# Expert outputs scattered to token rows, h1 kept in SBUF and the smallest experts last: one encoder block on one core

## The chip, the cores and the metric

The kernel runs on one core of one Trainium2 chip. The metric is the device time of one execution in microseconds (us), the median of three runs. An execution computes one layer for 512 tokens of width 1024, all in float32 (the large matmuls of the first half are done in three passes of a split format). Five engines run their own instruction streams and meet at semaphores: PE (matmul, with PEld, its weight loads), DVE (vector), ACT (scalar), POOL (GpSimd) and SP, which here only issues DMAs. DMAs are issued from the queues of SP, ACT and POOL and carried by the core's 16 DMA engines. PSUM holds matmul results, SBUF the working tiles (128 partitions), DRAM the inputs and two buffers of the kernel's own.

## The reference

Before the part that is changed: `h = LayerNorm(x)`, one projection, a gated MLP branch and a gated delta rule branch, and `h1 = LayerNorm(alpha*h + mix)`. What matters here is what follows:

```python
def _hier_moe(x, w_rg, b_rg, w_re, b_re, w1, w3, w2):      # x: h1, 512 x 1024
    pg = softmax(xt @ w_rg + b_rg); grp = argmax(pg, -1)    # 1 of 4 groups
    le = (xt @ w_re + b_re).reshape(n_tok, 4, 8)[own group] # 8 experts of it
    top_v, top_i = lax.top_k(le, 2)                         # 2 of the 8
    gate = p_grp * softmax(top_v, -1)
    ...
    def expert_block(xb, e):
        return (silu(xb @ w1[e]) * (xb @ w3[e])) @ w2[e]
    out = zeros.at[tok].add(gate * y)                       # sum of a token's 2 experts
h = LayerNorm(alpha * h1 + out)                             # LN2: the output
```

Both experts of a token lie in one group. There are 32 experts of 1024 x 512 (w1, w3) and 512 x 1024 (w2): 6.3 MB each. Which tokens an expert gets is data. Worked out from the reference's inputs, the 1024 pairs of token and expert fall very unevenly: two experts get none, the largest 130, 126, 104 and 94.

## The kernel before

**First half, to about 680 us.** Projections, gating and the delta rule (eight heads) are written through a recording layer (`Rec`) that sets the order by costs; all its instructions carry line 214. During the heads SP also fills `y_dram` (line 1519), the DRAM buffer for the experts' outputs, with zeros: 48 DMAs of 512 KB (lines 1578 to 1580). Then `out_ln1` (line 948) multiplies by `w_o`, adds the residual, normalizes without gain and bias, and writes these rows of h1 to `h1_dram`; the router (`Router`, lines 1044 to 1276) finds each token's two experts as the tiles come by.

**Order of the experts.** `Router.order` (line 1088) sets the order of the 32 blocks from the counts in the first 256 tokens: experts in a fixed sequence, those that look empty moved ahead of the last four. The first three are known beforehand. With these inputs the last four blocks have 126, 13, 130 and 19 tokens, and the two experts without tokens stand side by side as blocks 24 and 25.

**Experts.** `Experts.run` (line 1313) goes through the blocks, written out in full. Each expert's weights come as six loads of 1 MB on SP's queue (`load_big`, line 391) into a ring of 18 buffers `raw` (lines 1608 and 1621); a load is issued when its buffer is free, and is skipped by a condition where the expert has no token. For block b, in program order: POOL gathers the tokens of block b+2 from `h1_dram` by an indirect DMA (`fetch`, line 1394; 64 rows always, 96 more under an If); PE multiplies up (line 1447) in parts: a small one of up to 32 tokens and up to two of 64, each under an If; ACT and DVE form silu times product (lines 1454, 1455); PE turns the next block's tokens (line 1422); PE multiplies block b-1 down (line 1475); and `store_y` (line 1478) copies the results from PSUM (DVE the small part, line 1483; ACT the large ones, line 1485) and POOL stores them with five plain DMAs, each under a condition, to the expert's own 160 rows of `y_dram` (lines 1487, 1492). Stores to `y_dram` wait for one another where the framework sees that they could overlap. Between these steps `Router.rest` (line 1153) puts in DVE work for the gates, for places of outputs (`yi`) and for experts with over 160 tokens (`nov`, `oi`; none here).

**End.** `finish_rows` (line 1004) loads h1 again (4 x 512 KB) and the rows of gain and bias (4 x 512 KB) with SP, and forms alpha*h1 with gain and bias. A loop over overflow blocks follows (line 1661), which these inputs never enter. `finish` (line 1022) gathers the two expert rows of every token (8 indirect DMAs of 128 rows, line 1028), adds them with their gates (DVE, line 1034), normalizes (statistics in lines 357 to 375, then lines 1037 to 1039), and stores the four tiles of 128 tokens (line 1040).

Of the kernel before, what the change touches and what calls it, by code (L numbers as in the profile page):

```python
# [34 lines left out]
NYROW = (32 + 6) * NB + 64  # L35
# [5 lines left out]
NPRE = 3  # L41

# [217 lines left out]
class K:  # L260
# [4 lines left out]
    def consts(self, S, M, W):  # L265
# [78 lines left out]
        iota("eidnb", [128, E], [[NB, E]], 0, 0)  # L344
        iota("seq", [128, E], [[1, 8], [8, 4]], 0, 0)
# [6 lines left out]
        iota("tok", [128, NT], [[128, NT]], -2 * T, 1)  # L352
        c["tok16"] = S.tile([128, NT], F16, name="tok16")
# [650 lines left out]
    def finish_rows(self, h1_dram):  # L1004
# [6 lines left out]
        self.raws, self.nraw = free[8:14], 0  # L1011
# [10 lines left out]
    def finish(self, W, r, y_dram):  # L1022
        nc, a = self.nc, self.a
        v, act = nc.vector, nc.scalar
        ys = self.ys
        for t in range(NT):
            for k in range(2):
                nc.gpsimd.indirect_dma_start(out=ys[2 * t + k], out_offset=None, in_=y_dram,  # L1028
                                             in_offset=bass.IndirectOffsetOnAxis(ap=r.yi[:, k, t:t + 1], axis=0),
                                             bounds_check=NYROW - 1, oob_is_err=False)  # L1030
        for t in range(NT):
            f = self.h1f[t]
            for k in range(2):
                v.scalar_tensor_tensor(out=f, in0=ys[2 * t + k], scalar=r.g[:, t, k:k + 1], in1=f,  # L1034
                                       op0=OP.mult, op1=OP.add)
# [3 lines left out]
            (nc.gpsimd if t < 3 else v).tensor_tensor(out=f, in0=f, in1=self.l2b, op=OP.add)  # L1039
            nc.sync.dma_start(out=a["out"][t * 128:(t + 1) * 128, :], in_=f)  # L1040
# [3 lines left out]
class Router:  # L1044
# [3 lines left out]
    def __init__(self, nc, tc, S, W, P, cst, lg, persist):  # L1048
# [9 lines left out]
        self.idx = persist.tile([128, 2, E], I32, name="idx")  # L1058
        self.cum = S.tile([128, NT, E], F32, name="cum")
# [28 lines left out]
    def order(self):  # L1088
# [3 lines left out]
        for t in range(2):  # L1092
            q = W.tile([128, 2, E], BF, name="oq")
            v.tensor_tensor(out=q, in0=bc(cst["iota"][:, 0:E], 2, 1), in1=bc(self.ek[:, :, t], E, 2), op=OP.is_equal)
            for k in range(2):
                nc.tensor.matmul(self.cps[:, NT], cst["ones_bf"], q[:, k], start=t + k == 0, stop=t + k == 2)
        f = W.tile([128, E], F32, name="of_")
        v.tensor_scalar(f.rearrange("p (j g) -> p j g", g=4), self.cps[:, NT].rearrange("p (g j) -> p j g", g=4),
                        0.0, None, op0=OP.is_gt)
        v.memset(f[:, 0:NPRE], 1.0)  # L1100
        r = W.tile([128, E], F32, name="or_")
# [42 lines left out]
    def sort(self):  # L1144
        nc, v = self.nc, self.nc.vector
        for i, n in enumerate((NA, NB - NA)):
            v.tensor_scalar(self.idx[0:n, i], self.sps[i][0:n], 2.0 * T, None, op0=OP.add)
# [588 lines left out]
```

## Time and profile before

| | |
|---|---|
| median of 3 runs | 1244.05 us (1242.74 to 1249.01) |
| profiled execution, its own time | 1246.53 us |
| its span, first to last instruction | 1244.8 us |
| PE, DVE, ACT, POOL busy | 83%, 52%, 32%, 16% of the span |
| moved by DMA | 296.10 MB, mean 238 GB/s |

Times in the profile count from the start of the span. The page's 40 slices are 31 us each; a digit is a share in tenths. A view of stages (windows) has a row for each stretch of time: its length, the busy time of PE, PEld, DVE, ACT and POOL with the number of instructions, the granted PE clock, the busy share of the 16 DMA engines, and GB/s. A view of waits gives who waited for whom, the total in us, how often, and the longest. Groups of instructions name the line, engine, operation and tiles (out<-in), shape and count, then busy us and mean ns of one, then idle time ahead and what ended it. `raw` is the ring of weight buffers, which the end of the kernel reuses for h1, rows and gathered outputs.

### The profile page before, as it was taken

The numbers are of one execution on the slowest core, as the hardware profiler recorded it, in microseconds if no ns is written. First come the engines' busy times: TensorE is split into PE (matmuls) and PEld (weight loads), VectorE is DVE, ScalarE is ACT, GpSimd is POOL, SyncE is SP. The second block draws the span as 40 slices with busy tenths as digits, with TensorE's granted clock in tenths as the row PEclk, the third lists the DMA queues.
The fourth block names the chain that finished last, engine by engine and source line by source line (L and its number), as shares of the span: only waits on it lengthen the run. The fifth ranks groups of instructions, "written<-read, shape, count | busy, mean of one in ns | idle before, by whom it ended". The sixth has DMA issues, their size and how long they took to land. (4 is left out here: it accounts for less than half of the span.)

```text
span 1244.8 us, 19415 instructions
## 1 busy us (share of the span) xinstructions
PE 1039.3 (83%) x6880; PEld 687.0 (55%) x6880; DVE 646.2 (52%) x1356; ACT 403.1 (32%) x844; POOL 193.5 (16%) x377
## 2 busy tenths in 40 slices
PE   4999999999999999999999588787877586579810
PEld 2888788867777777667887333443333242234300
DVE  7566444567667777754865444533223232433246
ACT  6333355444555455435431311111111111211111
POOL 1000100212212132200001101111111101111043
PEclk9999999999999999999999698997979897799965
DMA  5422533899221121114672799999999999999832
GB/s 172 153 84 69 160 95 110 284 341 362 70 68 58 45 68 52 34 52 152 238 308 91 295 385 409 391 411 400 414 390 415 399 414 399 377 387 387 349 115 111
DMA packets 76899, 296.10 MB, mean 238 GB/s; under 512 B 9328, under 2 KB 34176, under 8 KB 53216
## 3 DMA queue, kind: packets, MB, share of 16 engines
q1 hardware_dynamic: 66672, 272.13, 58.0%
q0 software_dynamic: 7504, 17.20, 4.3%
q10 hardware_dynamic: 2592, 4.99, 1.2%
q8 instruction: 87, 1.43, 0.5%
q14 instruction: 44, 0.36, 0.1%
HBM read 277.36 MB, written 50.35 MB: 263 GB/s over the span
## 5 line engine op out<-in xcount | busy, mean ns | idle before, releaser
L214 PE MATMUL psi<-hTh,lo 128*128 128x512 f32 x448 | 183.0, 410 | 1.6 <-DVE lo L214 1.6
L214 PE MATMUL psi<-hTh,hi 128*128 128x512 f32 x448 | 183.5, 413 | 0.9 <-ACT hi L214 0.5
L214 PE MATMUL psi<-hTl,hi 128*128 128x512 f32 x448 | 183.1, 411 | 0.0
L1455 DVE TENSOR_TENSOR h<-h,u 128x640 f32<-128x640 f32 x32 | 26.3, 822 | 279.2 <-ACT h L1454 267.2
L214 DVE TENSOR_TENSOR lo<-raw,hi 128x1024 fp32r<-128x1024 f32 x74 | 91.3, 1234 | 79.6 <-ACT hi L214 78.9
L1447 PE MATMUL u<-raw,xs 128*32 128x256 f32 x1472 | 102.1, 426 | 29.8 <-DMA raw<-in_w 28.2
L214 ACT CAST hi<-raw 128x1024 fp32r<-128x1024 f32 x74 | 77.5, 1047 | 117.3 <-PE psi L214 100.2
L1447 PE MATMUL u<-raw,x 128*64 128x512 f32 x448 | 103.6, 618 | 5.9 <-PEq L1387 2.9
L214 PEld LDWEIGHTS psi<-hTh,lo 128*128 128x128 f32 x448 | 84.4, 188 | 21.3 <-issue 3.9
L214 PEld LDWEIGHTS psi<-hTh,hi 128*128 128x128 f32 x448 | 84.6, 189 | 20.3 <-issue 2.8
L214 PEld LDWEIGHTS psi<-hTl,hi 128*128 128x128 f32 x448 | 84.4, 189 | 17.2 <-issue 1.6
L1447 PEld LDWEIGHTS u<-raw,xs 128*32 128x32 f32 x1472 | 50.9, 120 | 73.4 <-DMA raw<-in_w 38.6
L1454 ACT ACTIVATE h<-u 128x640 f32<-128x640 f32 x32 | 22.6, 705 | 204.5 <-PEq L1389 160.9
L1447 PEld LDWEIGHTS u<-raw,x 128*64 128x64 f32 x448 | 35.5, 143 | 68.6 <-issue 60.0
L1475 PE MATMUL y<-raw,hT 128*64 128x512 f32 x224 | 60.1, 672 | 11.5 <-PEq L1387 9.2
L1475 PE MATMUL yz<-raw,hT 128*32 128x256 f32 x736 | 55.2, 437 | 16.4 <-PEq L1427 5.9
L1464 ACT COPY hT<-t 128x128 f32<-128x128 f32 x32 | 8.5, 266 | 184.0 <-PE t L1461 172.7
L1483 DVE COPY ysmall<-yz 32x256 f32<-32x256 f32 x128 | 53.3, 417 | 16.8 <-PE yz L1475 15.3
L214 DVE SCALAR_TENSOR_TENSOR acc<-xp,cols,acc 128x512 f32<-128x512 f32 x72 | 54.7, 760 | 4.7 <-ACT acc L214 3.5
L1492 POOL DMA_DIRECT2D y_dram<-ylarge x128 | 19.5, 155 | 194.1 <-DMA y_dram<-ysmall 114.8
L1475 PEld LDWEIGHTS yz<-raw,hT 128*32 128x32 f32 x736 | 26.3, 121 | 35.7 <-issue 18.0
L1422 PE MATMUL t<-ident,mh 64*128 64x64 f32 x256 | 23.5, 237 | 25.8 <-PEq L1389 20.0
(437 smaller groups left out, 1864.9 us busy)
## 6 DMA issues: line engine op xcount, KB each, us to landing
raw<-in_w SPq DMA_DIRECT2D x192, 1024.0 KB
raw<-in_wt SPq DMA_DIRECT2D x73, 512.0 KB
y_dram<-zero SPq DMA_DIRECT2D x48, 512.0 KB
y_dram<-ylarge POOLq DMA_DIRECT2D x128, 128.0 KB
raw<-in_wv SPq DMA_DIRECT2D x8, 512.0 KB
raw<-in_wo SPq DMA_DIRECT2D x4, 1024.0 KB
y_dram<-ysmall POOLq DMA_DIRECT2D x32, 128.0 KB
vt<-in_x SPq DMA_DIRECT2D x4, 512.0 KB
```

The source lines that it names most:

```text
L214: op._ins = getattr(getattr(self.nc, op.attr), op.name)(*map(real, op.args), **{k: real(x) for k, x in op.kw.items()})
L1422: nc.tensor.transpose(self.t[0][:, k * NA:k * NA + NA], r[0][:, k * 128:k * 128 + 128], ident[0:NA, 0:NA])
L1447: self.nc.tensor.matmul(self.u[q * r:(q + 1) * r, NP if p is None else p, 0:c], x[:, k, r0:r0 + r], self.raw[b, k // 2][:, o:o + c], start ...
L1454: self.nc.scalar.activation(out=h, in_=u[:, :, 0], func=AF.Silu)
L1455: self.nc.vector.tensor_mul(out=h, in0=h, in1=u[:, :, 1])
L1464: self.nc.scalar.copy(out=x[:, n], in_=self.t[1][:, 0:128])
L1475: self.nc.tensor.matmul(y[q * r:(q + 1) * r, 0:c], t[:, i, j * r:(j + 1) * r], self.raw[b, 4 + k // 2][:, o:o + c], start=k == 0, stop=k == 3)
L1483: nc.vector.tensor_copy(out=small[:, q], in_=self.y0[q * 32:(q + 1) * 32, 0:256])
L1492: nc.gpsimd.dma_start(out=dst[:, q * 512:(q + 1) * 512], in_=large[q * 64:(q + 1) * 64, p], cond=n > 32 + 64 * p)
```

## The change

**Places of rows.** The router now sorts pairs (token and slot, 2*512) instead of tokens; `rows` computes for each block the pair's row for the small part (`itail`) and for the large parts (`islot`), with an index out of bounds where there is no token.

**Stores.** `y_dram` becomes 1024 rows, two for each token side by side. `store_y` issues three indirect DMAs (scatters) from POOL, for every block and without conditions, and declares that no two have a row in common. `yo_dram` is used only in a fallback.

**Buffers.** The four tiles of h1 stay in SBUF; the second part of the ring shrinks from 9 to 8 buffers (17 in all), and from block 25 on four more are taken out for the tail. There is one landing buffer for large gathers instead of two, and the large gather of block b+2 is issued after the next block is turned.

**Order.** `Router.order` ranks by a key: experts that look empty come about ten places later than their turn, and the smallest expert of each group, by the counts of the first 256 tokens, goes to the end. With these inputs the last four blocks have 2, 18, 5 and 15 tokens; a token has no two of them, since they are of four groups. Their outputs are not stored: they are kept in one tile (`Y`) or read from PSUM.

**Tail.** From block 25 on, `Tail` does the end's work between the blocks' steps: gain and bias as 4 KB rows spread by PE, alpha*h1 with gain and bias, then at block 29 plain loads of `y_rows` (four of 1 MB, from ACT's queue, two rows of a token in one partition), the sums with gates, LN2 and the stores of all four tiles of 128 tokens, the tokens of the last four experts wrong in them. Those tokens (40 pairs here) are handled apart in a tile `F` of 128 rows: their h1 and their other expert's row are gathered, the last four outputs added, LN2 done, and their rows scattered over the output at the very end.

**Fallback.** A flag is the sum of three counts: two of the last four experts in one group, a last expert with over 32 tokens, an expert with over 160. If it is positive, an If loads `y_rows` over to `yo_dram`, runs the last four experts again with their stores, and ends as before. With these inputs it is 0.

**Zeros.** 8 DMAs of 512 KB instead of 48.

The diff, cut to its core:

```diff
@@ Router.order
+        mn = W.tile([128, 4], F32, name="om_")
+        v.tensor_reduce(out=mn, in_=gj(sc), axis=AX.X, op=OP.min)
...
+        v.scalar_tensor_tensor(out=f, in0=lt, scalar=128.0, in1=f, op0=OP.mult, op1=OP.add)
+        eq = W.tile([128, E, E], BF, name="oeq")
+        v.tensor_tensor(out=eq, in0=bc(f, E, 1), in1=bc(f, E, 2), op=OP.is_lt)
@@ Experts.run
         for b in range(nb + 1):
             if b + 2 < nb:
-                for i in range(2):
-                    self.fetch(b + 2, i)
+                self.fetch(b + 2, 0)
+            if tail and b >= RT:
+                tail(b, 0)
             if b < nb:
                 self.parts(b, self.up)
-                load(4)
+                if tail and b == RT:
...
+                    self.spare, kk.raws, kk.nraw = kk.raws[0:4], kk.raws[4:], 0
+                else:
+                    load(4)
                 self.gate(b)
...
-            if b:
-                self.store_y(b - 1)
+            if b and not (tail and b == nb):
+                self.store_y(b - 1, tail)
             next(more, None)
+            if tail and b >= RT:
+                tail(b, 1)
@@ Experts.store_y
+    def scatter(self, out, idx, src):
+        x = self.nc.gpsimd.indirect_dma_start(out=out, out_offset=bass.IndirectOffsetOnAxis(ap=idx, axis=0), in_=src,
+                                              in_offset=None, bounds_check=out.shape[0] - 1, oob_is_err=False)
...
+            self.tc.declare_no_dep(x.ins, group="rows", reason="no two have a row in common")
...
-        nc.gpsimd.dma_start(out=self.y_dram[ds(row + r0, 32), :], in_=small.rearrange("r q n -> r (q n)"), cond=d > 0)
+        self.scatter(self.y_dram, itail, small.rearrange("r q n -> r (q n)"))
         for p in range(NP):
-            for q in range(2):
-                nc.gpsimd.dma_start(out=dst[:, q * 512:(q + 1) * 512], in_=large[q * 64:(q + 1) * 64, p],
-                                    cond=n > 32 + 64 * p)
+            self.scatter(self.y_dram.rearrange("r (q n) -> (r q) n", q=2), islot[:, p], large[:, p])
@@ Tail.__call__ (new; RT = 25, E = 32)
+        elif (b, at) == (RT + 4, 0):
+            kk.behind(self.load(0), ex.stores)
+            self.load(1)
+        elif (b, at) == (RT + 4, 1):
+            self.add(0, 1)
+            self.load(2)
+            self.load(3)
+            self.gather(self.O, self.y_dram, r.lother, 2 * T)
+        elif (b, at) == (RT + 5, 0):
+            self.apply((0, 1), self.stats(0, 1))
+        elif (b, at) == (RT + 5, 1):
+            self.add(2, 3)
...
+        elif (b, at) == (RT + 6, 0):
+            self.m = self.stats(2, 3)
+        elif (b, at) == (RT + 6, 1):
+            self.apply((2, 3), self.m)
...
+        elif (b, at) == (E, 2):
...
+            (rs, mean), = self.stats(F)
+            self.norm(F, rs, mean)
+            x = g.indirect_dma_start(out=kk.a["out"], out_offset=bass.IndirectOffsetOnAxis(ap=r.lidx, axis=0), in_=F,
+                                     in_offset=None, bounds_check=T - 1, oob_is_err=False)
@@ build
-    close(OT, OP_, RP, OS, MM, RH, OH)
+    close(OT, OP_, RP, OS, MM, OH)
-    kk.add_raws(ER2, 9)
+    kk.add_raws(ER2, 8)
-    kk.finish_rows(h1_dram)
+    with tc.If(flag > 0):
+        kk.finish_rows(h1_dram, y_dram, yo_dram, ex.stores)
...
+    with tc.manual_schedule():
+        tail(E, 2)
```

Three places of the built programs show what moves. First POOL in the loop over the experts, from one block's stores to the next gathers, before (`mh` is the landing buffer of tokens, `cnti` the counts, ISA a condition):

```order
L1487 ISA
L1487 DMA y_dram<-ysmall 32x1024
L1492 ISA
L1492 DMA y_dram<-ylarge 64x512
L1401 DMA mh<-h_dram,idx 64x1024
L1380 TENSOR_LOAD cnti
L1398 COMPARE_AND_BRANCH
L1401 DMA mh<-h_dram,idx 96x1024
```

The same place now:

```order
L1549 DMA y_rows<-ysmall,itail 1024x1024
L1549 DMA y_rows<-ylarge,islot 2048x512 x2
L1468 DMA mh<-h_dram,idx 64x1024
L1454 UNCONDITIONAL_BRANCH
L1456 UNCONDITIONAL_BRANCH
L1494 UNCONDITIONAL_BRANCH
L1447 TENSOR_LOAD cnti
L1465 COMPARE_AND_BRANCH
L1468 DMA mh<-h_dram,idx 96x1024
```

The row of the conditioned large store stands four times in a block before; now there are three scatters without a condition, and the large gather has moved behind the turn of the next block (the branch of line 1494). Second, SP at the end of the experts, before, with the last weight load and what follows it:

```order
L1387 UNCONDITIONAL_BRANCH
L1389 UNCONDITIONAL_BRANCH
L399 ISA
L399 DMA raw_5392<-in_w 128x2048
L1013 DMA raw_5393<-h_dram 128x1024 x2
L1015 DMA raw_5395<-in_rows 128x1024 x2
L1659 TENSOR_LOAD nov
L1661 COMPARE_AND_BRANCH
L1040 DMA out<-raw_5393 128x1024 x2
```

And now (`h1s` are the tiles of h1):

```order
L401 DMA raw_5355<-in_w 128x2048
L401 ISA
L401 DMA raw_5356<-in_w 128x2048
L1691 DMA out<-h1s_4428 128x1024
L1691 DMA out<-h1s_4429 128x1024
L401 ISA
L401 DMA raw_5361<-in_w 128x2048
L1691 DMA out<-h1s_4430 128x1024
L1691 DMA out<-h1s_4431 128x1024
L1861 TENSOR_LOAD flag
L1862 COMPARE_AND_BRANCH
```

The loads of h1 and of the rows are gone from SP, and the stores of the output stand ahead of the flag, the first two of them ahead of the last weight load. Third, ACT's queue in the last blocks now, from the spread of LN2's rows on (before, ACT issued no DMA among the experts):

```order
L1648 ACTIVATE raw_5357<-t_5366 128x512
L1656 DMA raw_5359<-y_rows 128x2048
L1656 DMA raw_5360<-y_rows 128x2048
L1454 UNCONDITIONAL_BRANCH
L1456 UNCONDITIONAL_BRANCH
L1521 ACTIVATE h<-u 128x640
L1494 UNCONDITIONAL_BRANCH
L1465 UNCONDITIONAL_BRANCH
L1498 UNCONDITIONAL_BRANCH
L1531 COPY hT<-t_5366 128x128
L1532 COPY hT<-t_5365 128x512
```

The loads of the expert rows stand on ACT ahead of a block's silu (line 1521), so that ACT reaches the silu only when the scatters before them have landed.

More of the change, by code (lines that the diff above doesn't have):

```diff
@@ L1010, in finish_rows @@
         self.h1f, (g, b, self.l2g, self.l2b), self.ys = half[0:4], half[4:8], half[8:16]
-        self.raws, self.nraw = free[8:14], 0
+        self.raws, self.nraw = free[8:], 0
+        for i, y in enumerate(self.ys):
+            sl = slice(i * 128, (i + 1) * 128)
+            x = nc.sync.dma_start(out=y, in_=y_dram[sl, :])
+            if i == 0:
+                self.behind(x, stores)
+            nc.sync.dma_start(out=yo[sl, :], in_=y)
         for t in range(NT):
@@ L1344, in run @@
         next(more, None)
[L1345 to L1346 removed]
+        self.fetch(0, 1)
         next(more, None)
@@ L1476, in down, with late @@
                                       self.raw[b, 4 + k // 2][:, o:o + c], start=k == 0, stop=k == 3)
-    def store_y(self, b):
-        nc, row = self.nc, self.blocks[b][0]
-        small = self.yp.tile([32, 4, 256], F32, name="ysmall")
-        large = self.yp.tile([128, NP, 512], F32, name="ylarge")
+    def late(self, i):
+        return self.Y[32 * i:32 * i + 32].rearrange("r (q n) -> r q n", q=4)
+    def scatter(self, out, idx, src):
+        x = self.nc.gpsimd.indirect_dma_start(out=out, out_offset=bass.IndirectOffsetOnAxis(ap=idx, axis=0), in_=src,
+                                              in_offset=None, bounds_check=out.shape[0] - 1, oob_is_err=False)
+        if self.behind:
+            self.kk.behind(x, self.behind)
+            self.behind = None
+        if out.tensor.name == self.y_dram.tensor.name and not self.tracked:
+            self.tc.declare_no_dep(x.ins, group="rows", reason="no two have a row in common")
+            self.tc.add_to_no_dep_group("rows", x.ins)
+        self.stores.append(x)
@@ L1482, in store_y @@
+    def store_y(self, b, tail=None):
+        nc, (itail, islot) = self.nc, self.blocks[b][0]
+        i = b - (E - NL)
+        late = tail and i >= 0
+        small = self.late(i) if late else self.yp.tile([32, 4, 256], F32, name="ysmall")
         for q in range(4):
             nc.vector.tensor_copy(out=small[:, q], in_=self.y0[q * 32:(q + 1) * 32, 0:256])
+        if late:
+            return
+        large = self.yp.tile([128, NP, 512], F32, name="ylarge")
         for p in range(NP):
             nc.scalar.copy(out=large[:, p], in_=self.y[p])
-        n, d, r0 = (self.n(b, ET.Pool, i) for i in range(3))
```

336 lines of the change are left out of this document (237 added, 99 removed).

## The prediction

> **What bounds the kernel now.** I read the page's slices first, then the stages, the waits, the chain. The slices:
>
> ```profile
> PE   4999999999999999999999588787877586579810
> DMA  5422533899221121114672799999999999999832
> ```
>
> Up to slice 22 PE is full; from slice 24 to slice 37 DMA stands at 9 and PE below it. Then both go, while the execution lasts two slices more. The stages (columns as told above):
>
> ```profile
> 682.00:696.00 14.00, 9.40 (x57) 7.32 (x56) 6.43 (x24) 2.78 (x6) 0.86 (x2) 0.91 1.01 418
> 732.00:1050.00 318.00, 246.19 (x2303) 115.08 (x2300) 116.11 (x243) 52.97 (x105) 46.60 (x131) 0.89 1.02 405
> 1050.00:1070.00 20.00, 12.65 (x86) 5.30 (x82) 7.32 (x14) 3.77 (x8) 2.57 (x12) 0.89 0.87 339
> 1165.00:1175.00 10.00, 6.85 (x113) 4.32 (x108) 4.14 (x10) 2.53 (x5) 0.51 (x1) 0.99 1.02 408
> 1175.00:1180.00 5.00, 5.00 (x35) 1.94 (x29) 2.08 (x5) 0.00 (x0) 0.67 (x5) 0.68 0.49 195
> 1180.00:1200.00 20.00, 7.34 (x61) 2.73 (x55) 5.17 (x7) 4.80 (x8) 2.81 (x9) 0.80 0.19 43
> 1200.00:1245.00 45.00, 0.00 (x0) 0.00 (x0) 30.78 (x38) 4.96 (x4) 23.07 (x15) 0.50 0.40 140
> ```
>
> The experts from 732 us on run at the pace of their weights: DMA 1.02, 405 GB/s, PE 246 of 318 us. An expert has 6.29 MB, so 15.5 us. PE needs far less where an expert has up to 32 tokens, as its up and down show, and more for the large ones (two large parts):
>
> ```profile
> 1129.83 3.66 PE L1447 MATMUL u<-raw,xs 128*32 128x256 f32 x64
> 1164.46 1.93 PE L1475 MATMUL yz<-raw,hT 128*32 128x256 f32 x32 [0.42 <-PEq L1427]
> 1149.44 13.95 PE L1447 MATMUL u<-raw,x 128*64 128x512 f32 x64
> 1177.15 7.59 PE L1475 MATMUL y<-raw,hT 128*64 128x512 f32 x32
> 1185.40 1.93 PE L1475 MATMUL yz<-raw,hT 128*32 128x256 f32 x32
> ```
>
> So a small block is 5.6 us of PE and a large one 27; only a large block at the very end puts PE after the stream. The last load of weights landed at about 1167: DMA is full to 1175 and for 49% of the next 5 us, to 1177.4, and the last that it carries are the loads of h1 and of the rows, queued on SP behind the weights:
>
> ```profile
> 1151.16 8.98 SPq L1013 DMA_DIRECT2D raw<-h_dram  x4
> 1162.32 7.83 SPq L1015 DMA_DIRECT2D raw<-in_rows  x4
> raw<-h_dram SPq DMA_DIRECT2D x4, 512.0 KB
> ```
>
> Eight of half a MB are 4.19 MB, 10.3 us at 405, so the weights were in at 1167.1. The 77.7 us after that are PE's rest of the block of 130 tokens, to 1187.3 (the last of the matmul rows), then the chain of waits:
>
> ```profile
> 1187.54 10.02 DMA y_dram<-ylarge
> 1204.80 6.04 DMA raw<-y_dram,yi
> 1237.83 1.23 DVE raw L1039
> ```
>
> A wait until stores have landed, gathers of all outputs, LN2 of four tiles, a store. So the end of the profile is set first by the stream's bytes, then by what hangs on the last expert's outputs.
>
> **The change part by part.** I sum when the weights have landed now, and what follows them.
>
> *Bytes in the stream.*
>
> ```profile
> q0 software_dynamic: 7504, 17.20, 4.3%
> DA<-g_dram POOLq DMA_DIRECT2D x8, 256.0 KB
> raw<-in_w SPq DMA_DIRECT2D x192, 1024.0 KB
> ```
>
> Loads run ahead of PE by as many buffers as the ring has, so one fewer (17, not 18) is 1 MB less in SBUF when the experts start: +1.05 MB. The four taken out at block 25 cost no bytes, since 13 MB ahead of PE is still two experts. The four plain loads of `y_rows` come at blocks 29 and 30, while weights still flow, on ACT's queue but through the same 16 engines: +4.19. Two of four output stores stand ahead of the last weight load: +1.05. The gathers for the 40 apart pairs, two of 4 KB each: +0.33. Stores fall: POOL's queue moved 17.20 MB, less 2.10 (`DA`), 4.19 (1024 tokens gathered) and 4.19 (8 end gathers) leaves 6.7 MB of stores, whole parts of 32 or 64 rows, 0.86 of it after 1180 (43 GB/s for 20 us); now only 984 real rows go, 4.03 MB: −1.8. Together +4.8 MB; at 405 GB/s 11.9 us. The loads of h1 and rows lay behind the weights and go for nothing. Weights have landed at 1167.1 + 11.9 = **1179.0**.
>
> The rate itself is bound by two rows: 339 GB/s in a stretch with stores, 418 in one without. If scatters left no mark, the 447 us from 732 to 1179 would become 433 (× 405/418, −14); if they marked it twice as much, +14. I take none, since the same rows go to the same memory in both kernels. The Trainium skill ("DMA: Bandwidth & Descriptors", Where 436 GB/s comes from) says that for transfers between HBM and SBUF the HBM side binds at about 358 GB/s; by it the 4.8 MB would be 13.4 us, 1.5 more. The trace disagrees: 405 for 318 us with one core at work.
>
> *Order.* All blocks from 26 on are at most 18 tokens, so PE, 5.6 us of 15.5, waits for weights when the last land. PE's 20 us behind them go. Those large blocks now stand as blocks 22 and 24, and PE's arrears there (27 − 15.5 us each) are absorbed within three small blocks.
>
> *POOL.* Three scatters take the place of five conditioned stores per block. Rows for their price:
>
> ```profile
> L1401 POOL DMA_INDIRECT mh<-h_dram,idx x38: 931/986/1457, 699.7 to 1140.2; - x38
> L1028 POOL DMA_INDIRECT raw<-y_dram,yi x8: 989/1458/2068, 1200.2 to 1212.2; - x8
> POOL y_dram L1492 <- DMA y_dram<-ysmall: 114.8, 19, 9.3
> ```
>
> Scatters at 1 to 2 us are 3 to 6 us per block, gathers 2 to 3, of 15.5; the 115 us in which POOL waited for stores goes, but they lay beside a stream that set the pace. The large gather, moved behind the next block's turn, has still more than a block of time. Cost 0 while that cover lasts; without it, rival 2.
>
> *Zeros, router.* 40 of 48 zero DMAs go from 214 to 307 us:
>
> ```profile
> 214.00:307.00 93.00, 90.28 (x495) 68.06 (x494) 56.16 (x116) 41.58 (x96) 19.89 (x29) 1.00 0.96 324
> 640.00:682.00 42.00, 40.95 (x220) 31.56 (x219) 23.03 (x87) 7.51 (x11) 4.06 (x4) 1.00 0.39 140
> ```
>
> PE is busy 90.3 of those 93 us, so at best 2.7 us come from it; I take 0, as DVE and ACT end PE's waits there. The router's order chain is some 2.6 us longer on DVE, which has 19 of 42 us free: 0, at most +2.
>
> *Tail between blocks.* The sums, statistics and norms of four tiles are the DVE work of the old end:
>
> ```profile
> L1034 DVE SCALAR_TENSOR_TENSOR raw<-raw,g,raw 128x1024 f32<-128x1024 f32 x8 | 10.0, 1269 | 3.8 <-DMA raw<-y_dram,yi 3.8
> L362 DVE BATCH_NORM_STATS2 st<-raw 128x6 f32<-128x512 f32 x8 | 5.4, 683 | 0.0
> L372 POOL TENSOR_TENSOR rs<-ve,mhalf 128x1 f32<-128x1 f32 x4 | 3.2, 802 | 5.7 <-DVE ve L370 4.2 <-ACT raw L1037 1.5
> L368 DVE BATCH_NORM_AGGREGATE mv<-st 128x2 f32<-128x12 f32 x4 | 0.8, 204 | 0.1
> L370 DVE TENSOR_SCALAR ve<-mv 128x1 f32<-128x1 f32 x4 | 0.6, 151 | 0.1
> L1483 DVE COPY ysmall<-yz 32x256 f32<-32x256 f32 x12 | 5.0, 418 | 10.4 <-PE yz L1475 10.3
> ```
>
> Per tile 2.5 + 1.4 + 0.4 and two full-width operations of 1.23 (the chain's last row): 6.8 us, 14 for the two tiles loaded last, and a block's own DVE work is at most 5.7 (116 us for 20.5 blocks from 732 to 1050): some 20. The last two loads stand behind block 29's steps; a block and a half of stream, some 23 us, is left then. It fits, barely; what is over is added at the end (rival 1).
>
> *End chain*, from the last weights: half of a down 1.0 (of 1.93); the flag's If, nearest row the old loop's branch, from POOL's wake at 1197.57 to its next work:
>
> ```profile
> 1197.57 0.09 POOLq L1661
> 1199.35 0.03 POOLq L1028
> ```
>
> 1.8, and five engines must meet: I take 2.5 (1 to 5). Four sums of 32 rows by 256 at 0.42: 1.7. Statistics 2 × 0.68 + 0.20 + 0.15: 1.7. Two full-width operations of 1.23, POOL's power (0.55 to 0.8) beside the first: 2.6. Last a scatter of `F`; the old end took 5.7 us from DVE's last instruction (1239.06) to the span's end, issue of SP, landing and exit; POOL's issue is longer than SP's: 6.5. The scatter also waits for the stores of the last two tiles (1.05 MB, 2.6 us behind the weights), which land in the 9.5 us ahead of it. Sum **16.0**; 1179.0 + 16.0 = 1195.0. The profiled execution has 1.73 us outside its span (1246.53 against 1244.8) and is 2.5 above the median, so 1196.7 profiled and **1194** median, 50 us or 4% under 1244. (0.5%, 6 us, is about what a measurement of this kernel can tell from no change.)
>
> **The rivals.**
> *1, the tail shows:* ACT stands at the loads of `y_rows` until all scatters landed, with silu of that block behind it, PE and DVE behind silu; a store's wait at the end of before was 10 us. If loads come one block's step later, or DVE's 20 us start late, the last tiles' stores and `F` follow 10 to 20 us behind the weights: 1204 to 1214. For it: the 23 us against 20. Against: PE has 10 us to spare per block.
> *2, POOL bounds:* three scatters without condition on every block. A block's 15.5 us less 2.6 for gathers leaves 12.9: above 4.3 us a scatter POOL sets the pace. To lose the 50 us over the 28 blocks from 732 on takes 1.8 us more a block, so 4.9 a scatter; at 5 a block takes 17.6, 2.1 more, 59 in all: 1253, slower than before. The rows say 1 to 2 us. The Trainium skill ("SBUF — State Buffer", SBUF: two separate sides) says that a DMA issued by GpSimd waits for its descriptors while DVE holds the shared port, 620 ns becoming about 3100. Three at that price would be 9.3 us, still under 12.9; the trace, whose gathers ran beside DVE's sums at 0.99 to 2.07, shows nothing of that size.
> *3, the stream itself runs faster* with fewer and unchained stores, at 418: −14, 1180.
> *4, it doesn't do what it says:* the flag comes out positive and four experts run again (24 MB, 62 us), 8.4 MB are copied (20), stores wait (10), the old end follows (37): 1310. My count from the inputs gives 2, 18, 5, 15 and four groups, flag 0.
>
> **How the numbers follow.** Forecast 0.66, 1187 to 1208 (half of the rate's −14, all of its +14); rival 1 0.18; rival 2 0.04, a quarter of it within 0.5% of before; rival 3 0.10; rival 4 0.02. The low end is rival 3 with the zeros' 2.7 and the flag's 1.5: 1176. The high end is rival 1's 1214 with the flag's 2.5 and the router's 2: 1219. Faster by over 0.5%: 0.94; same 0.01; slower 0.05 (rivals 2 and 4).
>
> **What would show it.** Right: the stages from 732 on again at 395 to 410 GB/s; the last `in_w` wait of PE at 1176 to 1182, PE's last matmul within 2 us of it; POOL's scatters at 1 to 2 us and POOL without a wait for stores; 14 to 18 us from the last matmul to the end, the flag's wait and one scatter among them. Wrong: DVE or ACT work of the four tiles ending after the last matmul (rival 1); weight loads with idle DMA between them, and scatters above 4 us (rival 2); above 415 GB/s (rival 3); weight loads behind the flag (rival 4). A stream of another rate would make every stage right and the time wrong.

## The result, and the profile after

The changed kernel takes 1211.23 us (median of 4 runs, 1208.06 to 1211.85), before 1245.05 in the same comparison: ratio 0.972, 95% interval 0.9689 to 0.9751. That is faster by 2.8%; the forecast was 1194, range 1176 to 1219. The profiled execution took 1211.33 us, its span is 1209.6, where the forecast had 1195.0.

The slices of the page, after:

```profile
span 1209.6 us, 18970 instructions
PE   3999999999999999989999868786788888898753
DMA  4422332612122112111566579999899999999995
```

DMA stands at 9 to slice 39 now, so the quiet end of before is gone; but there is an 8 in slice 29, and PE is higher than before in most slices from 30 to 36. The stages of after (length, busy time of PE, PEld, DVE, ACT, POOL, granted PE clock, DMA share, GB/s):

```profile
214.00:307.00 93.00, 90.14 (x487) 67.98 (x485) 56.22 (x114) 40.81 (x94) 19.30 (x29) 1.00 0.35 114
732.00:1050.00 318.00, 256.69 (x2186) 119.01 (x2186) 122.80 (x256) 55.28 (x109) 92.64 (x95) 0.91 1.00 386
...
842.00:872.00 30.00, 21.86 (x126) 10.40 (x125) 9.33 (x19) 4.90 (x9) 7.77 (x8) 0.83 0.80 286
...
680.00:1193.00 513.00, 402.23 (x3419) 187.92 (x3417) 221.06 (x478) 91.11 (x176) 129.55 (x133) 0.86 0.97 379
1084.00:1094.00 10.00, 9.30 (x99) 4.25 (x95) 1.34 (x2) 2.53 (x5) 3.87 (x4) 1.00 0.64 229
```

The same two stretches before, the first of them up to the last weights there:

```profile
680.00:1169.00 489.00, 373.44 (x3279) 177.57 (x3281) 178.05 (x392) 86.53 (x170) 67.77 (x186) 0.88 0.99 392
842.00:872.00 30.00, 20.67 (x198) 10.29 (x192) 11.46 (x22) 5.16 (x10) 5.35 (x13) 0.77 1.02 399
```

The forecast had 405 GB/s from 732 to the last weights. It is 386 to 1050, and there are two holes that before does not have (it has one of its own, 3 us from 1050 to 1070): from 842 to 872 DMA is at 0.80 (against 1.02 in full work: 6.6 us lost), from 1084 to 1094 at 0.64 (3.8 us). The weights therefore land late, as the timeline of the last matmuls and of the end chain shows:

```profile
1193.62 1.93 PE L1542 MATMUL yz<-raw,hT 128*32 128x256 f32 x16 [2.21 <-DMA raw<-in_w]
...
1197.31 2.00 DVE L1628 SCALAR_TENSOR_TENSOR raw<-yz,lgate,raw 32x256 f32<-32x256 f32 x4 [1.45 <-DVEq L1862]
1199.34 1.29 DVE L1671 BATCH_NORM_STATS2 te<-raw 128x6 f32<-128x512 f32 x2
...
1201.20 1.46 POOL L1680 TENSOR_TENSOR tr<-tv,mhalf 128x1 f32<-128x1 f32 x1 [16.51 <-DVE tv L1677]
1202.69 1.28 DVE L1686 SCALAR_TENSOR_TENSOR raw<-raw,tr,raw 128x1024 f32<-128x1024 f32 x1 [0.44 <-POOL tr L1680]
1204.27 1.05 POOL L1632 DMA_INDIRECT out<-raw,lidx  x1 [1.61 <-DVE raw L1686]
```

PE waits for weights up to 1193.6, not 1179.0: 14.6 us late. From there to the end are 16.0 us: the end chain is as long as forecast. So the miss of the profiled execution, 14.6 us, lies in the stream of weights, and the question of the experiments was why it is slower.

Who waits for weights answers a part of it. PE's and PEld's waits for `in_w` from 732 to 985, before (total us, times, longest):

```profile
PE u L1447 <- DMA raw<-in_w: 17.3, 13, 3.8
PEld u L1447 <- DMA raw<-in_w: 24.6, 13, 4.3
```

and after:

```profile
PE y L1542 <- DMA raw<-in_w: 2.6, 1, 2.6
PEld u L1514 <- DMA raw<-in_w: 0.6, 2, 0.3
```

Before, PE stood and waited for weights in that stretch; now it hardly ever does. For 250 us PE is more often the late one: from 732 to 985 SP waits 84 us in sum for PE, before 30. Up to 842 and from 872 to 1050 the DMA engines stay full all the same (share 1.02); between these two times they do not. SP's own waits from 835 to 872 in the changed kernel, in which its loads wait until PE has freed a buffer:

```profile
SPq L401 <- PE u L1514: 11.8, 4, 9.2
SPq L401 <- DMA raw<-in_w: 8.0, 3, 3.6
SPq L401 <- PEq L1456: 7.0, 4, 3.7
```

In the same stretch of before SP waits only for earlier loads (27.4 us, 13 times).

### The profile page after: what moved, and what is told of

Read it like the earlier page. It is cut to its first block, busy times and chain, and to the rows that moved or that the text cites. A ratio compares the mean times of both kernels' runs of the same rounds, so it can differ in the third digit from the quotient of the medians.

```text
span 1209.6 us, 18970 instructions
## 1 busy us (share of the span) xinstructions
PE 1054.7 (87%) x6896; PEld 690.3 (57%) x6896; DVE 660.2 (55%) x1399; ACT 397.6 (33%) x837; POOL 229.5 (19%) x296
## 2 busy tenths in 40 slices
DMA packets 57931, 268.82 MB, mean 222 GB/s; under 512 B 12882, under 2 KB 17266, under 8 KB 33737
## 3 DMA queue, kind: packets, MB, share of 16 engines
q8 instruction: 87, 1.43, 0.5%
## 5 line engine op out<-in xcount | busy, mean ns | idle before, releaser
L1514 PE MATMUL u<-raw,xs 128*32 128x256 f32 x1472 | 98.3, 420 | 20.5 <-DMA raw<-in_w 18.9
L1542 PE MATMUL yz<-raw,hT 128*32 128x256 f32 x736 | 60.6, 464 | 17.3 <-DMA raw<-in_w 6.6
L1549 POOL DMA_INDIRECT y_rows<-ysmall,itail x28 | 26.1, 931 | 229.3 <-DVE ysmall L1565 207.1
L1549 POOL DMA_INDIRECT y_rows<-ylarge,islot x56 | 57.7, 1030 | 48.8 <-ACT ylarge L1570 35.7
L1542 PE MATMUL y<-raw,hT 128*64 128x512 f32 x224 | 57.3, 653 | 7.7 <-PEq L1454 4.9
L1565 DVE COPY ysmall<-yz 32x256 f32<-32x256 f32 x112 | 46.7, 417 | 7.1 <-PE yz L1542 5.1
```

Source lines behind the costliest of these rows:

```text
L1514: self.nc.tensor.matmul(self.u[q * r:(q + 1) * r, NP if p is None else p, 0:c], x[:, k, r0:r0 + r], self.raw[b, k // 2][:, o:o + c], start ...
L1542: self.nc.tensor.matmul(y[q * r:(q + 1) * r, 0:c], t[:, i, j * r:(j + 1) * r], self.raw[b, 4 + k // 2][:, o:o + c], start=k == 0, stop=k == 3)
L1549: x = self.nc.gpsimd.indirect_dma_start(out=out, out_offset=bass.IndirectOffsetOnAxis(ap=idx, axis=0), in_=src, in_offset=None, bounds_che ...
L1565: nc.vector.tensor_copy(out=small[:, q], in_=self.y0[q * 32:(q + 1) * 32, 0:256])
```

## The experiments

Three theories stood at the start: the ring fills behind a late PE, because of the empty experts (A) or because the light blocks are missing early (B); or the loads run at a lower rate beside the scatters, with or without idle time (C). D and E were formed on the way; each expectation says what they hold. Ratios are to the kernel before, in one comparison each, with 95% intervals; the changed kernel has 0.972 (0.9689 to 0.9751). Two kernels whose times differ by up to some 5 us are not told apart by these intervals; where a verdict rests on the trace, its row is shown, and that is one execution of each kernel.

### First four: which place, and what fills the ring

**The empty experts later.**

```diff
-        v.scalar_tensor_tensor(out=f, in0=f, scalar=-10.5, in1=cst["seq"], op0=OP.mult, op1=OP.add)
+        v.scalar_tensor_tensor(out=f, in0=f, scalar=-18.5, in1=cst["seq"], op0=OP.mult, op1=OP.add)
```

> The changed kernel with one number of the order's key altered (-18.5 for -10.5), so that the two experts without tokens stand as blocks 16 and 18 instead of 10 and 12. The changed kernel's weights land at 1193.2, 14 us later than forecast; its DMA engines stand partly idle from 842 to 870 (5.8 us lost) and from 1084 to 1094 (3.6 us), which the forecast did not have. Theory A (an expert without tokens loads nothing but takes six buffers of the ring, 12 of 17 for two that stand close, while PE is 20 to 30 us behind the loads): the idle time of 842 to 870 goes, up to 3 us come back at the new place, where PE is nearer to the loads: 3 to 6 us faster than the changed kernel, ratio to before 0.968 to 0.970. Theory B (the light blocks that went to the end are missed early, so PE's arrears last and the ring is full whatever the empty experts do): idle time of the same size moves to another place, within 2 us of the changed kernel, 0.971 to 0.974. Theory C (the rate of the loads is lower because of the scatters, idle or not): no change, 0.972.

Measured: 1207.6 us, ratio 0.971 (0.9684 to 0.9736). The stages of this kernel:

```profile
842.00:872.00 30.00, 25.46 (x196) 12.39 (x197) 8.90 (x19) 4.80 (x9) 8.74 (x9) 0.94 1.02 396
940.00:950.00 10.00, 4.50 (x58) 3.02 (x59) 5.77 (x12) 2.53 (x5) 3.88 (x4) 0.87 0.82 320
1080.00:1092.00 12.00, 11.18 (x125) 5.49 (x125) 2.92 (x5) 2.53 (x5) 4.92 (x5) 1.00 0.56 195
```

The hole at 842 to 872 is gone (1.02), 2 us of it are back where the empty experts now stand (940 to 950), and the second hole has grown from 3.8 to 5.5 us. So the empty experts make the place of the first hole, as theory A says; the median is 3.6 us lower (1.2 by the ratios), at the edge of what was expected and not clear of noise.

**The heavy experts later.**

```diff
+        hv = W.tile([128, E], F32, name="oh_")
+        v.tensor_scalar(hv, self.cps[:, NT], 39.5, 8.0, op0=OP.is_ge, op1=OP.mult)
+        h2 = W.tile([128, E], F32, name="oh2")
+        v.tensor_scalar(h2, self.cps[:, NT], 60.0, -8.0, op0=OP.is_ge, op1=OP.mult)
+        v.tensor_tensor(out=hv, in0=hv, in1=h2, op=OP.add)
+        v.tensor_tensor(out=f, in0=f, in1=hv, op=OP.add)
```

> The changed kernel with the experts of 82, 104 and 94 tokens put about eight places later by the order's key, so that small blocks come earlier; the two empty experts stand as blocks 9 and 10, side by side. Theory B (PE's arrears): PE has caught up with the loads by about 850, the idle DMA time of 842 to 870 (5.8 us) goes, some may come where the heavy blocks now stand: 3 to 6 us faster than the changed kernel, 0.968 to 0.970 of before. Theory A (empty experts take the ring's buffers): the two side by side still leave 5 of 17 buffers for weights while PE is some 19 us behind, idle time of 4 to 6 us stays at about 830 to 850: within 2 us of the changed kernel. Theory C: no change.

Measured: 1183.8 us, but the shift of 8.0 made keys equal, so that blocks were left without their experts and their loads and work are missing (260.54 MB moved, against 268.82 in the changed kernel). This time says nothing on the theories; the edit stands again below, with keys that differ.

**One ring buffer fewer.**

```diff
-    kk.add_raws(ER2, 8)
+    kk.add_raws(ER2, 7)
```

> The changed kernel with one ring buffer fewer (16, from block 25 on 12). Theories A and B (the ring is full in the places where DMA idles): one load less ahead costs 2.6 us at the start (1.05 MB at 405 GB/s) and 2.6 us more at each of the two places of idle time: 6 to 10 us slower than the changed kernel, 0.977 to 0.980 of before. Theory C (the lost time is a lower rate under scatters): 2.6 us alone, 0.974.

Measured: 1214.5 us, 0.9754 (0.9729 to 0.9778), 3.2 us above the changed kernel. The hole at 842 to 872 is as deep as in the changed kernel (0.81 against 0.80). Both theories of a full ring had 6 to 10 us, C had 2.6: the median is nearest to the one load that comes less early, but the interval, up to 0.9778, does not rule out 6 us.

**Half of the rows.**

```diff
-        return self.nc.scalar.dma_start(out=self.y[t % 2], in_=self.y_dram[t * 256:(t + 1) * 256, :].rearrange(
-            "(p k) n -> p (k n)", k=2))
+        return self.nc.scalar.dma_start(out=self.y[t % 2][:, 0:D], in_=self.y_dram[t * 256:(t + 1) * 256, :].rearrange(
+            "(p k) n -> p (k n)", k=2)[:, 0:D])
```

> The changed kernel, but of the expert rows each plain load brings only the first of a token's two (2.10 MB instead of 4.19; the second is left out of the sum, the rest is as before). Forecast's term: these loads share the weights' bandwidth, so 2.10 MB less are 5.2 us at 405 GB/s: 5 us faster, 0.968 of before. Rival: the tail's work on DVE sets the end behind the weights anyway, or the loads go in gaps: 0 to 2 us faster, 0.970 to 0.972.

Measured: 1208.3 us, 0.9712 (0.9677 to 0.9746): 2.9 us faster by the medians, 1.0 by the ratios. The interval holds the forecast's term (5.2) and the rival (0 to 2) alike, so the time does not decide between them. In the traces the last down, which waits for the last weights, starts at 1190.6 against 1193.6: 3.0 us for bytes that take 5.2.

### Second four: PE or the rate

**The heavy experts later, keys apart.** The edit as above with 8.25 in place of 8.0.

> The changed kernel with the experts of 82, 104 and 94 tokens really put later (by 8.25 in the key, so that no two keys are equal): blocks 12, 17 and 21; the empty experts are blocks 9 and 10. Theory D (formed after the first runs: up to block 24 PE, not the loads, is the longer of two nearly equal sums; it lags, the ring fills, and DMA idles where empty experts or the shrinking of the ring leave few buffers; the order only chooses where): the idle time of 842 to 870 goes and comes back at the heavy blocks' new place just ahead of the shrinking (1080 to 1100): within 2 us of the changed kernel, 0.970 to 0.974 of before. Theory B (arrears of the early blocks alone): 3 to 6 us faster, 0.968 to 0.970.

Measured: 1219.9 us, 0.9796 (0.9766 to 0.9826). Two of its stages:

```profile
842.00:872.00 30.00, 22.96 (x226) 13.21 (x226) 11.43 (x22) 4.36 (x9) 8.43 (x9) 0.89 1.02 405
...
1080.00:1102.00 22.00, 17.64 (x160) 7.49 (x149) 5.55 (x10) 2.53 (x5) 6.26 (x8) 0.84 0.26 89
```

The first hole goes and a larger one opens just ahead of the tail (0.26 for 22 us, 17 us lost), as theory D said of the place; the size, 9 us slower, neither theory had. Nor is the cause D's alone: from 1040 to 1180 SP waits once for 20.8 us for a load of the tail's rows (`in_rows`), of which more below.

**The ring shrinks at block 27.**

```diff
-                if tail and b == RT:
+                if tail and b == RT + 2:
...
-        if (b, at) == (RT, 1):
+        if (b, at) == (RT + 2, 1):
...
-        elif (b, at) == (RT + 1, 1):
+        elif (b, at) == (RT + 3, 0):
             self.spread(self.rows[0:2], ALPHA)
-        elif b == RT + 2:
-            self.affine(self.f[2 * at:2 * at + 2])
-        elif (b, at) == (RT + 3, 0):
-            self.affine([self.F])
         elif (b, at) == (RT + 3, 1):
+            self.affine(self.f + [self.F])
             self.spread(self.rows[2:4], 1.0)
```

> The changed kernel with the four ring buffers taken out at block 27 instead of 25 (the tail's first steps are pressed into blocks 27 and 28). Theory D: the second idle place (1084 to 1094, 3.6 us) is due to the ring's fall to 13 while PE is still behind with the 126 and 130 tokens of blocks 22 and 24; two small blocks later PE has caught up: that idle time goes, weights land 3 to 5 us sooner, ratio to before 0.968 to 0.970. Rival: PE would be behind there with 17 buffers too and the idle time stays: 0.972; or the pressed tail ends later: 0.974 or more.

Measured: 1226.1 us, 0.9847 (0.9818 to 0.9875), 15 us slower. The hole moved to where the tail now begins (DMA 0.47 from 1120 to 1132), and there SP waits, by name, for the tail's loads of rows (11.5 us). Theory D's expectation failed. That name led to theory E.

**PE with less work.**

```diff
-        for k in range(KD):
+        m = KD if p is None else KD // 2
+        for k in range(m):
```

> The changed kernel, where the large parts' up does only half of its matmuls (the other half of the sum is left out), about 49 us less of PE in 14 large parts, all else as it was. Theory D (DMA idles since PE lags): idle time of 842 to 870 and of 1084 to 1094 goes, weights land 9 to 11 us sooner, at 1182 to 1184; ratio to before 0.963 to 0.966. Theory A (only the empty experts' buffers): some of the idle time at 842 to 870 stays. Theory C (rate under scatters): the loads are the bound anyway, 0 to 2 us, 0.970 to 0.972.

Measured: 1207.8 us, 0.9696 (0.9675 to 0.9716). Its stages:

```profile
680.00:1193.00 513.00, 374.75 (x3211) 177.63 (x3211) 224.16 (x482) 90.85 (x176) 127.87 (x133) 0.81 0.97 380
842.00:872.00 30.00, 24.31 (x155) 11.23 (x159) 10.86 (x22) 6.80 (x14) 11.10 (x12) 0.82 0.96 353
1078.00:1090.00 12.00, 10.87 (x101) 4.37 (x97) 1.63 (x3) 1.83 (x4) 3.61 (x4) 0.99 0.50 169
```

With less PE work the first hole shrinks from 6.6 to 1.8 us, so PE's lag is its cause together with the empty experts' buffers. The second stays (6.2 us), so halving these matmuls does not touch its cause. PE did not become 49 us shorter: its busy time from 680 to 1193 fell by 27 us (402.23 to 374.75), since the granted clock there was 0.81 and not 0.86 and the other matmuls took longer (a small part's up 446 ns in the mean, against 420). The time gained 3.5 us by the medians, which is not clear of noise.

**No rows stored.**

```diff
-        v.scalar_tensor_tensor(out=slot, in0=m, scalar=-OOB, in1=y, op0=OP.mult, op1=OP.add)
+        v.scalar_tensor_tensor(out=slot, in0=m, scalar=0.0, in1=y, op0=OP.mult, op1=OP.add)
...
-        v.tensor_tensor(out=tail, in0=t[:, 1], in1=x[0:32, 0], op=OP.add)
+        v.scalar_tensor_tensor(out=tail, in0=t[:, 1], scalar=OOB, in1=x[0:32, 0], op0=OP.add, op1=OP.add)
```

> The changed kernel with all indices of the scatters in the loop out of bounds, so that POOL issues as many scatters but no expert output is stored (the output lacks them). 4.03 MB less to move. Theory C (scatters cost more than their bytes, by a lower rate): bytes 10.0 us at 405 GB/s and the 5 us by which the busy rate fell short of before (400 against 404 GB/s): 13 us or more, 0.961 or less. Theory D: where PE lags the loads can't use the room, so less than the bytes: 5 to 8 us, 0.965 to 0.968, with more idle DMA time than the changed kernel's 26 us from 680 on.

Measured: 1223.1 us, 0.9812 (0.9785 to 0.984): with 4 MB less to move it is 12 us slower. Both theories fail. (Its expert outputs are left out of the result.) The profile of this kernel, one stage and what SP waited for from 1060 to 1120:

```profile
1084.00:1112.00 28.00, 23.24 (x242) 11.25 (x242) 9.76 (x19) 4.36 (x9) 7.34 (x8) 0.88 0.13 43
```

```profile
SPq L401 <- DMA raw<-in_rows: 28.8, 1, 28.8
SPq L401 <- DMA raw<-in_w: 20.0, 5, 8.8
```

For 28 us the DMA engines do next to nothing (0.13), since a weight load waits for a load of 4 KB. The program and the trace tell why: the loads of SP and ACT take their completion semaphores in turn from the same eight. The four rows are issued by ACT behind the copies of block 24's outputs; the weight load that comes next on such a semaphore cannot be issued until the row has landed. In the changed kernel the timeline of the queues shows the same, smaller:

```profile
1081.84 11.83 SPq L401 DMA_DIRECT2D raw<-in_w  x5
1089.25 0.49 ACTq L1593 DMA_DIRECT2D raw<-in_rows  x1
```

The first row of the fence is a group: its first load goes out at 1081.84, its second only at 1090.93, on the semaphore of the 4 KB row that ACT issued at 1089.25. That is the second hole, and it says why an edit that delays PE around block 24 (heavy experts later, 20.8 us) makes it longer.

### Last four: the tail's loads on another queue, and the order alone

**The tail's loads from POOL.**

```diff
-                act.dma_start(out=x, in_=kk.a["rows"][row:row + 1, :])
+                g.dma_start(out=x, in_=kk.a["rows"][row:row + 1, :])
...
-        return self.nc.scalar.dma_start(out=self.y[t % 2], in_=self.y_dram[t * 256:(t + 1) * 256, :].rearrange(
+        return self.nc.gpsimd.dma_start(out=self.y[t % 2], in_=self.y_dram[t * 256:(t + 1) * 256, :].rearrange(
```

> The changed kernel with the tail's plain loads (four rows of 4 KB, four loads of y_rows) issued from POOL's queue instead of ACT's; nothing else. Theory E (formed after the second runs: the loads of SP and ACT take their completion semaphores in turn from the same eight, so a weight load on SP that comes next on a semaphore waits until a load of ACT's has landed that ACT issues only when PE's block is done; the profile names the rows as what SP waited for 7.7 us in the changed kernel, 20.8, 11.5 and 28.8 us in the three runs that were slower than expected): SP no longer waits for the rows, the idle DMA time of 1084 to 1094 (3.6 us) goes and weights land 3 to 5 us sooner, ratio to before 0.968 to 0.970. Theory D (PE's lag and the smaller ring): SP waits for PE there instead, the idle time stays, 0.972. If POOL's loads hold up its scatters or the tail: 0.974 or more.

Measured: 1220.2 us, 0.9815 (0.9786 to 0.9844): 9 us slower, against theory E's 2 to 5 faster. Its stages, and the loads of `y_rows`:

```profile
842.00:872.00 30.00, 25.73 (x162) 12.75 (x161) 11.56 (x22) 4.66 (x10) 8.74 (x9) 0.83 0.82 293
1084.00:1094.00 10.00, 5.23 (x76) 3.45 (x72) 2.64 (x6) 1.46 (x3) 3.87 (x4) 0.78 1.02 411
1094.00:1130.00 36.00, 32.22 (x266) 14.26 (x262) 14.46 (x23) 7.46 (x14) 13.47 (x14) 0.78 0.94 367
```

```profile
L1656 POOL DMA_DIRECT2D raw<-y_rows x4: 540/556/600, 1155.9 to 1174.0; - x4
```

What theory E says of the hole is right: SP no longer waits for rows and DMA is at 1.02 from 1084 to 1094. Of the 3.8 us, though, 2.9 come back from 1094 to 1130 (0.94), so the cause of the hole is shown, and what its removal is worth is not. And the kernel is late for another reason, and it is late before the edit can act: PE starts block 20 at 995.1, in the changed kernel at 981.1, though PE's instructions stand in the same order, row for row, in both programs. The difference is PE's wait at one branch, the end of a block's Ifs (line 1456), ahead of the transposes. From 732 to 1100 in the changed kernel:

```profile
PE t L1489 <- PEq L1456: 15.5, 21, 3.4
```

and in this one:

```profile
PE t L1489 <- PEq L1456: 40.0, 20, 4.3
```

PE lags by what it waits there, and the loads of `y_rows` start 15 us later than in the changed kernel (1155.9 against 1140.9). The weights are not late here: DMA works in full to 1185 and at 0.41 from 1185 to 1205. But PE stands 13 us in the last blocks behind DVE, which is busy with the tail:

```profile
1183.55 0.48 PE L1528 MATMUL t<-ident,h 128*128 128x128 f32 x1 [13.25 <-DVEq L1498]
```

The tail of four tiles then ends at 1203.9, after the last matmul (1202.4): rival 1 of the forecast, in an experiment.

The times of the other runs go with this wait, with one exception; that does not show by itself that the wait makes the time, since three of the slower kernels also have the larger holes told above. The wait at that branch is 15.0 us with the empty experts later, 15.0 with half of the rows, 19.1 with a ring of 16: these three took 1208 to 1214 us. It is 26.1 (heavy experts later), 27.4 (shrink at 27), 34.8 (no rows stored), 40.0 (here), 37.7 and 40.7 (next two): these took 1216 to 1226. With half of PE's large up, the exception, it is 32.8, with 27 us less PE time, at 1208. So the edits of the second group changed, besides what they were meant to, how long PE stands at its branches; their times against the changed kernel cannot be put down to the edit alone.

**Both edits:** -18.5 in the key, and the tail's loads from POOL.

> Both edits: the empty experts as blocks 16 and 18, and the tail's loads on POOL's queue. Theories A and E together: the two idle places go, some 9 us of 14, less 2 us that stay near 945: weights land at 1184 to 1187, ratio to before 0.963 to 0.967. If the two idle places have one cause (PE's lag), the second edit adds nothing to the first: 0.970.

Measured: 1221.5 us, 0.9794 (0.977 to 0.9819). The branch's wait is 37.7 us; for the question of two holes or one it is inconclusive.

**No rows stored, and the tail's loads from POOL.** Both edits as above.

> As the kernel with all scatters out of bounds (no output of an expert is stored), and the tail's loads on POOL's queue. Theory E: that kernel was slower, against both expectations, because SP waited 28.8 us for a row load of ACT's; without it the 4.03 MB less show: 5 to 10 us faster than the changed kernel with its loads on POOL, 0.960 to 0.965 of before. Theory C (scatters lower the rate by more than their bytes): 13 us or more faster than that kernel, 0.958 or less. If out-of-bounds scatters cost time of their own: slower than the changed kernel again, above 0.975.

Measured: 1216.2 us, 0.9773 (0.9748 to 0.9798), 4.0 us under the kernel with loads on POOL, which has the same wait at the branch (40.7 here, 40.0 there), so that these two can be compared. The stretch without DMA after 1084 is gone, as theory E says. The six runs of each kernel (1213.2 to 1223.0 here, 1217.6 to 1227.6 there) leave some 0 to 10 us for 4.03 MB less: theory C's 13 us or more is not borne out, and the 10 us that the bytes alone would take stand at the edge. The median is less than half of that, which fits a stretch in which PE is often the late one, but does not show it. The ratio lies above 0.975, the place for scatters out of bounds that cost time of their own; they cost POOL what the others cost (1.01 us in the median), and the kernel on POOL with stored rows is slower still.

**The order alone, in the kernel before.**

```diff
-        iota("seq", [128, E], [[1, 8], [8, 4]], 0, 0)
+        iota("seq", [128, E], [[1, 4], [4, 8]], 0, 0)
+        iota("jx", [128, E], [[0, 4], [1, 8]], 0, 0)
...
-        v.tensor_scalar(f.rearrange("p (j g) -> p j g", g=4), self.cps[:, NT].rearrange("p (g j) -> p j g", g=4),
+        gj = lambda x: x.rearrange("p (g j) -> p g j", g=4)
...
```

(and so on through `Router.order`, which is the changed kernel's from here to its end).

> The kernel before with the changed kernel's order of experts alone (small ones last, the empty ones as blocks 10 and 12); stores, ring of 18, h1 loads and end as before. Forecast's term: PE's rest of 20 us behind the weights (1167 to 1187) goes down to about 2, the wait for stores and the end stay, the empty experts' idle time of about 6 us comes in: 10 to 16 us faster than before, 0.987 to 0.992. Rival: the order is worth nothing without the other parts, since the wait for stores or the loads of h1 and rows (to 1177) take the place of PE's rest: 0.996 to 1.0.

Measured: 1241.2 us, 0.9967 (0.9955 to 0.998), 4 us faster, the rival's case. One stage of it and the longest piece of its chain of waits:

```profile
842.00:872.00 30.00, 23.11 (x156) 11.20 (x153) 10.60 (x21) 4.69 (x10) 5.55 (x14) 0.89 0.93 338
```

```profile
1179.48 12.01 DMA y_dram<-ylarge
```

PE's rest behind the weights is gone: its last matmul ends at 1176.7, before at 1187.3. But the first gather of the end starts only 6.0 us sooner (1194.13 against 1200.18). The wait for stores, which stood at 1187.54 with 10.02 us, now stands at 1179.48 with 12.01; PE's rest had hidden a part of it, and the weights land 6 us later (1175 against 1169, by the records of the DMA packets). And the hole at 842 to 872 is there (0.93, 2.7 us) with a ring of 18, with the old stores and zeros: the order brings it.

## Why the prediction was right in its direction and late by 17 us

The time lies in the stated range, but above the 1187 to 1208 that the forecast's own case had. The range reached to 1219 for rival 1, a late tail, and that is not what happened here: the tail ended before the last matmul. That the range held is in this part luck.

- *Bytes in the stream.* Right in kind, too large. DMA moved 191.91 MB from 680 to 1169 before and 194.32 MB from 680 to 1193 after: 2.4 MB more, some 6 us, where the sum had 4.8 MB and 11.9 us. By the packets' records, 1.05 MB of h1 had landed ahead of the last weights before, which the sum did not count, and the weights still to come at 680 were 178.3 MB, before 179.1, where the sum had one load more.
- *That the stream sets the pace from 732 to its end:* this is the step that failed. The sum put POOL at 0, took from the order only PE's 20 us at the end, and held that PE's arrears at blocks 22 and 24 "are absorbed", on blocks of 5.6 us of PE. That figure leaves out what lies between matmuls: turns, branches and gates. The small experts that went to the end were blocks in which PE caught up; the empty ones, as blocks 10 and 12, bring no loads and hold twelve of 17 buffers, and PE hardly waits for weights until 985. From 842 to 872 DMA then waits for PE. By the packets' records the last weights landed at 1169 before (worked out as 1167.1) and at 1193 after. Of these 24 us, some 6 are bytes; some 10.5 are time without work (0.99 of 489 us busy, now 0.97 of 513); the rest, near 7, is a lower rate in full work. Against the forecast's 1179 that is 2 us for a landing worked out too early, 6 us less for bytes, and some 17 us of idle time and lower rate that the sum did not have. These parts are estimates from shares that are rounded to a hundredth, so each is good to a few us.
- *"The four taken out at block 25 cost no bytes".* Right for bytes, but what happens there was overlooked: the tail's row loads on ACT share the eight semaphores with SP's weight loads, and the stream stands 3.8 us. The text spoke of ACT waiting for scatters; it had not looked at SP waiting for ACT.
- *The rate.* The sum bounded it by ±14 us and took none. Weights came 14.6 us late, and the two holes are 10.4 of it. The lower rate in full work stands mainly in the middle of the blocks. From 872 to 1000, in turn before, before with the order alone, the changed kernel, and the changed kernel with no rows stored:

```profile
872.00:1000.00 128.00, 97.30 (x899) 43.21 (x897) 36.64 (x71) 17.83 (x35) 17.41 (x49) 0.87 1.02 404
872.00:1000.00 128.00, 101.39 (x1024) 51.42 (x1024) 50.28 (x98) 25.27 (x50) 21.12 (x58) 0.89 1.02 404
872.00:1000.00 128.00, 104.55 (x1018) 50.04 (x1018) 48.81 (x96) 25.02 (x49) 42.10 (x43) 0.87 1.02 392
872.00:1000.00 128.00, 99.18 (x929) 49.23 (x933) 44.43 (x87) 22.10 (x44) 34.02 (x36) 0.83 1.01 391
```

  In these traces the lower rate comes neither with the order nor with the stored bytes. Which other part of the change brings it, the scatters as they are issued among them, is open.
- *PE's 20 us behind the weights* go, as said: the last down begins when its weights land.
- *POOL.* Right, by these rows of after:

```profile
L1549 POOL DMA_INDIRECT y_rows<-ylarge,islot x56: 984/1012/1997, 733.1 to 1134.0; - x56
L1549 POOL DMA_INDIRECT y_rows<-ysmall,itail x28: 881/891/1626, 731.9 to 1131.5; - x28
```

  Three scatters are 2.9 us of a block; rival 2 needed 4.3 each. The Trainium skill ("SBUF — State Buffer", SBUF: two separate sides) has about 3.1 us for a DMA issued by GpSimd that overlaps a copy on DVE. The longest scatter here is 2.0.
- *Zeros* are worth nothing: PE is busy 90.14 of the 93 us from 214 to 307, before 90.28. The experts begin 1.8 us earlier (703.00 against 704.78), so the router's longer chain does not show.
- *Tail between blocks.* It fits barely, as said: the last full-width operation of the four tiles ends at 1194.7, the last matmul at 1195.6. Delayed by 15 us (loads from POOL), it shows.
- *End chain:* 16.0 forecast, 16.0 measured. In it the last down is 1.9 and not 1.0, the flag 1.8 and not 2.5, the scatter to the end 5.3 and not 6.5; these errors cancel, so the agreement to a tenth is luck, and the size is right.
- *Median and profiled execution:* 0.1 us apart here, not 2.5; this is 2.4 of the 17 us.

No version clearly faster than the changed kernel was found; the lowest time of a kernel that leaves nothing out, 1207.6 us with the empty experts as blocks 16 and 18, has a ratio within the changed kernel's interval. A version with the empty experts later and the tail's four rows loaded ahead of the experts, so that SP meets no semaphore of theirs, was not tried.

## What to carry to other kernels

Where two engines' sums are nearly equal, taking the light blocks away from one end of an order makes the other resource the bound at that end: count the blocks' whole time, gaps and branches included, and run the ring forward block by block, before a stage is called bound by its loads. A load of a few KB on another queue can hold up the main stream if both take their completion semaphores from one set in turn, so look at what stands ahead of each on its own engine. And when an edit changes the time the wrong way, check first that the part of the trace ahead of the edit is still the same.

## What the runs showed of the hardware that was not expected

PE's wait behind a skipped part of a block, with the same order of instructions, was 0.7 us in the mean in one program (at most 3.4) and 2.0 in another (at most 4.3), 13 to 41 us in sum from 732 to 1100 over all the kernels. The wait was traced once for each program; the times stay with the program: the six runs of the kernel with loads on POOL are all slower than each of the four of the changed kernel. The Trainium skill ("Runtime: NRT & Kernel Launch", Instruction fetch mechanics) says that a taken branch whose target is not among the two pages held forces a fetch of that page before execution goes on. The trace has instruction transfers (87 on queue 8, 1.43 MB in all, as many in the kernel with loads on POOL) and a wait of this kind behind a taken branch; it does not show that the one is the cause of the other, nor why one program waits longer. That stays open.

A scatter of 128 rows whose indices are all out of bounds costs POOL as much as one that stores (median 1.01 us in both kernels, 0.89 for 32 rows).
